# Banded attention's last output projection split by key heads around the last weighing, and the last but one unit weighed ahead of the last turns

## The chip, the cores and the metric

The kernel runs on 1 core of one Trainium2 chip. The metric is the device time of the whole program in microseconds (us). Names of engines in the profile: PE is TensorE (PEld its weight loads), DVE is VectorE, ACT is ScalarE, POOL is GpSimd, SP is SyncE, which here only issues DMAs. Each engine works off its own list of instructions, one after the other; instructions wait on semaphores for results of other engines.

## The reference

A two layer transformer on 512 tokens of width 1024, in f32. Layer 0 has differential attention, layer 1 banded attention with sinks (window 128, 16 query heads in groups of 4 on 4 key heads), and each is followed by a SwiGLU of hidden width 2816. The change lies where layer 1's attention ends and its SwiGLU begins:

```python
p = e / (jnp.sum(e, axis=-1, keepdims=True) + jnp.exp(sink - m))
o = jnp.einsum('bnhgqk,bnkhd->bnqhgd', p.astype(vw.dtype), vw)
return o.reshape(B, S, SW_HEADS * HEAD_DIM) @ w_o
...
        x = x + swiglu(rms_norm(x, ffn_norm[l]), w_gate_up[l], w_down[l])
```

## The kernel before

**Products in three passes.** Every f32 operand is split into a rounded half `hi` (an ACT cast) and the rest `lo` (a DVE subtraction), and a product is three matmuls: hi by hi, hi by lo, lo by hi (`mm3`, L295 to L298). `split_evac` (L300) does that for a PSUM result: `ph`/`pl`, `oh`/`ol`, `hTh`/`hTl` are such pairs.

**Tiling.** The 512 tokens are four tiles t = 0 to 3 of 128. Banded attention is done in 16 units; a unit is one token tile with one key head (four query heads). Units 14 and 15 belong to token tile 3, with key heads 2 and 3. A unit has five steps: `turn_q` (transpose the queries), `score` (scores, softmax; L1395), `turn_p` for two key blocks (L1432: four PE transposes of the weights `s` into a `tr` bank, then ACT's `ph` and DVE's `pl`), and `weigh` (L1445: 12 matmuls of 256 columns into the only `po` bank, six for each key block, then `oh` by ACT and `ol` by DVE). `po` has one bank, so a weighing cannot start before the `ol` of the one ahead of it has read it.

**Output projection.** `o_block` (L457) adds one token tile's share of `o @ w_o` to the residual `xs`: for each of two column halves n it runs j = 0 to 3 (three matmuls of 512 columns each) into one `acc` bank and then adds the bank to `xs` on DVE (L468). j = 0 and 1 read the `oh`/`ol` of one unit, j = 2 and 3 those of the next: in the last call (`o_sw(1, 3)`, chunk 1, token tile 3) j = 0, 1 are unit 14's and j = 2, 3 are unit 15's. Its weights are four units of two `hi`/`lo` tiles, which fill the eight buffers that the pool has (`HLB`, L44).

**The SwiGLU's start.** `ffn.norm(t)` (L520) squares `xs` on ACT with a row sum (`xn<-xs`, L526), takes the inverse root on DVE by a chain of tiny instructions (`fss`, `rsq`, `frr`) and scales into `xn` (L532). `ffn.turn(t)` (L535) transposes `xn` in two banks of four PE transposes (L314) and splits each into the token tile's columns of `hTh`/`hTl`. `ffn.start` (L594) loads gate and up weights of the first column block: four `raw` loads of 512 KB by SP into two `raw` buffers (`RAWB`, L43), each split into two `hi`/`lo` pairs (ACT L269, DVE L270), the third load waiting until the first buffer has been split. Then come the products of tokens 0 to 255 with `hTh`/`hTl` (256 columns, so token tiles 0 and 1), later those of tokens 256 to 511; `turn(2)` and `turn(3)` stand ahead of the second and the fourth group of 24 matmuls.

**Order of the work.** PE's list is in the order of the code (`manual_schedule`). The steps of units are sorted by the times in `SW_AT` (L117), and projections of finished tiles fill between them (`fill.pull`, L1510). What is left of the fill comes at `fill.drain()` (L1521), then the last projection with `ffn.turn(0)` after its second and `ffn.turn(1)` after its sixth of eight (n, j) steps, then `ffn.start`. The lists of ACT, DVE and SP are put in order by a scheduler with priorities: `high_priority(offset=HOT)` moves the norm and the additions to `xs` far forward, the splits less far.

Of the kernel before, what the change touches and what calls it, by code (L numbers as in the profile page):

```python
# [13 lines left out]
ALU = mybir.AluOpType  # L14
# [26 lines left out]
HOT = 1220  # L41
# [72 lines left out]

DA_FILL3 = 0.4757
SW_K = [11.4, 13, 18.5, 22]
SW_AT = [11.99, 12, 15.9293, 17.8936, 24.5, 15.49, 15.5, 20.5, 21.3936, 26, 19.99, 20, 25, 26, 28.8496, 24.49, 24.5, 29.5, 30.5, 33.0389, 25.6, 29.3765, 35.7519, 36, 38.8496, 28.8, 30.9738, 38.2, 40.3017, 42.0496, 32, 34.1738, 41.4, 43.5017, 45.2496, 36.9539, 39.3779, 46.3539, 48.4383, 50.2036, 45.6745, 48.0985, 55.0745, 57.0527, 58.1744, 47.0802, 52.5434, 56.4802, 57.4802, 60.3298, 50.3802, 54.7802, 59.7802, 60.7802, 63.6298, 53.6802, 58.0802, 63.0802, 64.0802, 66.9298, 57.032, 60.327, 66.3802, 67.3802, 70.2298, 60.4435, 63.7903, 69.8435, 70.8435, 72.7553, 65.4286, 69.8286, 74.8286, 75.8286, 77.7403, 67.7612, 72.1612, 77.6383, 78.1612, 80.073]  # L117
SW_R = [24.5925, 29, 34.7335, 50, 54, 60.3794]
SW_F = 57.2488
SW_BOOST = 51  # L120
# [17 lines left out]
def tile_yoco_hybrid(  # L138
# [24 lines left out]
    nc = tc.nc  # L163
    count = [0]

    def nm(s):
        count[0] += 1
        return f"{s}_{count[0]}"
# [12 lines left out]
    def acc():  # L181
        return ps.tile([P, 512], F32, name=nm("acc"), tag="acc", bufs=4)

    def att(tag="tr"):
        return ps.tile([P, 512], F32, name=nm(tag), tag=tag, bufs=3 if tag == "tr" else 1)
# [7 lines left out]
    xs = xp.tile([P, NT, D], F32, name="xs")  # L193
# [101 lines left out]
    def mm3(dst, sh, sl, mh, ml, start, stop):  # L295
        nc.tensor.matmul(dst, sh, mh, start=start, stop=False)  # L296
        nc.tensor.matmul(dst, sh, ml, start=False, stop=False)  # L297
        nc.tensor.matmul(dst, sl, mh, start=False, stop=stop)  # L298

    def split_evac(hi, lo, src):  # L300
        with tc.high_priority(offset=pri["evac"]):
            nc.scalar.copy(hi, src)
            nc.vector.tensor_tensor(lo, src, hi.bitcast(F32), op=ALU.subtract)

    def new_hT():
        hh = xp.tile([P, KT, S], F32R, name=nm("hTh"), tag="hTh", bufs=1)
        hl = xp.tile([P, KT, S], F32R, name=nm("hTl"), tag="hTl", bufs=1)
        return hh, hl

    def transpose_in(hT, src, t, h):  # L310
        pt = att()
        for j in range(4):
            k = 4 * h + j
            nc.tensor.transpose(pt[:, j * P:(j + 1) * P], src[:, k * P:(k + 1) * P], ident)  # L314
        sl = (slice(None), slice(4 * h, 4 * h + 4), slice(t * P, (t + 1) * P))
        split_evac(hT[0][sl], hT[1][sl], pt.rearrange("p (j q) -> p j q", q=P))
# [112 lines left out]
    def q_evac(ap, pt):  # L429
        q = [ap.tile([P, 256], F32R, name=nm("q"), tag=f"q{z}", bufs=QB) for z in "hl"]  # L430
        split_evac(*q, pt[:, 0:256])
        return q
# [19 lines left out]
    def o_units(w, k0):  # L452
        wv = w.rearrange("(k p) n -> p k n", p=P)
        return {(j, n): load_w([wv[:, k0 + j:k0 + j + 2, n * 512:(n + 1) * 512]], 2, 512)
                for j in (0, 2) for n in range(2)}

    def o_block(units, pieces, t, ready=None):  # L457
        while ready and not ready():
            yield None
        for n in range(2):  # L460
            pt = acc()
            for j in range(4):
                sh, sl = pieces(j, t)
                mm3(pt, sh, sl, *units[j - j % 2, n].row(j % 2), j == 0, j == 3)
                yield 0.65
            xsl = xs[:, t, n * 512:(n + 1) * 512]
            with tc.high_priority(offset=HOT):
                nc.vector.tensor_tensor(xsl, xsl, pt, op=ALU.add)  # L468


    class Flow:
# [521 lines left out]
    class Pair:  # L993
# [105 lines left out]
        def turn(self, i, h):  # L1099
            hf = i // 2  # L1100
            if (hf, h) not in self.aT:
                self.aT[hf, h] = [[self.ap.tile([P, 2, 256], F32R, name=nm("aT"), tag=f"aT{e}", bufs=4)
                                   for _ in range(1 + hf)] for e in range(2)]
            th, tl = self.aT[hf, h]
            pt = att()
            src = self.sb[i][h]
            for j in range(i + 1):
                nc.tensor.transpose(pt[:, j * P:(j + 1) * P], src[:, 0, j * P:(j + 1) * P], ident)
            for jp in range(0, i + 1, 2):
                w = min(2, i + 1 - jp)  # L1110
                sl = (slice(None), slice(0, w), slice((i % 2) * P, (i % 2) * P + P))
                split_evac(th[jp // 2][sl], tl[jp // 2][sl],
                           pt[:, jp * P:(jp + w) * P].rearrange("p (j q) -> p j q", q=P))

        def weigh(self, hf, h):
            if h == 0:
                self.po = att("po")
            po, vs = self.po, self.vs
            th, tl = self.aT[hf, h]
            nj = 2 + 2 * hf  # L1120
            for j in range(nj):
                c0 = P if j == nj - 1 else 0
                mm3(po[:, h * 256 + c0:(h + 1) * 256],
                    vs[j][0][:, h * P:(h + 1) * P], vs[j][1][:, h * P:(h + 1) * P],
                    th[j // 2][:, j % 2, c0:256], tl[j // 2][:, j % 2, c0:256], j == 0, j == nj - 1)
            if h == 1:
                self.osb = self.ap.tile([P, 512], F32, name=nm("osb"), tag="osb", bufs=1)
                with tc.high_priority(offset=pri["evac"]):
                    nc.scalar.copy(self.osb, po)
                self.osq = self.ap.tile([P, 512], F32, name=nm("osq"), tag="u", bufs=3)  # L1130
                nc.scalar.activation(self.osq, self.osb, AF.Square)
# [29 lines left out]
    with tc.tile_pool(name="da", bufs=1, reuse_waits="tile") as ap:  # L1161
# [84 lines left out]
        for p in range(4):  # L1246
# [8 lines left out]
            else:  # L1255
                fill = Fill([o_da(0, range(NT)), o_da(1, range(2), lambda: 0 in pairs[3].outs)])
                each = DA_FILL3
                ffn = Ffn(0, ap)
# [34 lines left out]
    with tc.tile_pool(name="sw", bufs=1, reuse_waits="tile") as ap:  # L1293
# [92 lines left out]
        def place(u):  # L1386
            i, kk = divmod(u - 8, 2) if u >= 8 else (u % 4, 0)
            s, kv = ("C", 2 + kk) if u >= 8 else ("AB"[u // 4], u // 4)
            return s, i, kk, kv, ((i - 1, i) if i else (0,))
# [37 lines left out]
                nc.scalar.activation(sb[:, g, 0:n], sb[:, g, 0:n], AF.Copy, scale=rs[:, g:g + 1])  # L1427
            soft[u] = sb

        pT, soft, kdone, vdone = {}, {}, set(), set()  # L1430

        def turn_p(u, b):  # L1432
            s, i, kk, kv, blocks = place(u)
            if b >= len(blocks):
                return
            pt = att()
            for g in range(4):
                col = (g % 2) * 256 + (g // 2) * P
                nc.tensor.transpose(pt[:, col:col + P], soft[u][:, g, b * P:(b + 1) * P], ident)
            ph = ap.tile([P, 512], F32R, name=nm("ph"), tag="ph", bufs=2)  # L1440
            pl = ap.tile([P, 512], F32R, name=nm("pl"), tag="pl", bufs=2)
            split_evac(ph, pl, pt)
            pT[u, b] = (ph, pl)

        def weigh(u):  # L1445
# [16 lines left out]
        def pieces_sw(ch):  # L1462
            return lambda j, t: tuple(z[:, j % 2, :] for z in o_all[2 * ch + j // 2, t])

        sw_units = {}

        def o_sw(ch, t):
            while (2 * ch + 1, t) not in o_all:
                yield None
            if ch not in sw_units:  # L1470
                sw_units[ch] = o_units(sw_w_o[0], 4 * ch)
            yield from o_block(sw_units[ch], pieces_sw(ch), t)
            if ch:
                ffn.norm(t)

        def hook(k, t):
# [22 lines left out]
        todo = [(at, t, turn_a) for t, at in enumerate(SW_K)]  # L1499
        for u in range(16):  # L1500
            for n, f in enumerate((turn_q, score, turn_p, turn_p, weigh)):
                if u >= 4 or n:
                    todo.append((SW_AT[5 * u + n], u, f) + ((n - 2,) if n in (2, 3) else ()))
        todo += [(at, *z, q_rope) for at, z in zip(SW_R, (("B", 1), ("B", 2), ("B", 3), ("C", 1), ("C", 2), ("C", 3)))]
        todo.append((SW_F, Ffn))
        fill = Fill([gemm(units_of((wqv, 256, gq), (wkv, 256, gkv)), hT, 512, 2, b_post),
                     gemm(units_of((wqv, 512, gq)), hT, 512, 2, c_post)]
                    + [o_sw(0, t) for t in range(NT)] + [o_sw(1, t) for t in range(NT - 1)])
        now = 0.0
        for at, *z in sorted(todo, key=lambda z: z[0]):  # L1510
            fill.pull(at - now)
            now = at
            if z[0] is Ffn:
                ffn = Ffn(1, ap)
# [4 lines left out]
            else:  # L1519
                z[1](z[0], *z[2:])  # L1520
        fill.drain()  # L1521
        for n, _ in enumerate(o_sw(1, 3)):
            if n == 1:
                ffn.turn(0)
            if n == 5:
                ffn.turn(1)
        ffn.start({1: lambda: ffn.turn(2), 3: lambda: ffn.turn(3)})

    with tc.tile_pool(name="ffn1", bufs=1, reuse_waits="tile") as fp:
# [37 lines left out]
```

## Time and profile before

| | |
|---|---|
| median of 3 runs | 1122.76 us (1122.44 to 1123.15) |
| the profiled execution's own time | 1122.68 us |
| its span, first to last instruction | 1120.6 us |
| what lies around the span | 2.08 us |
| mean granted TensorE clock | 0.998 |
| busy: PE, DVE, ACT | 1101.9, 1007.9, 709.4 us |

The profile shows one execution. A row of a timeline has the start in us from the span's start, the time of the instruction (of several together, with x4), the engine, the line, the operation with out<-in, and in brackets how long the engine stood idle before it and what ended that. A matmul's time overlaps the next one's: what a matmul costs on PE is the distance of the starts.

### The profile page before, as it was taken

The page shows a single profiled execution, that of the slowest core. Times are in us where ns is not written, and L with a number is a line of the kernel's source. Part 1 is how long each engine was busy: PE and PEld are TensorE (multiplying, and loading weights), DVE is VectorE, ACT ScalarE, POOL GpSimd, SP SyncE. Part 2 cuts the span into 40 slices and gives each one's busy share as a digit, 9 for nine tenths or more (in the row PEclk, how much of TensorE's full clock was granted, in tenths as well). Part 3 has the DMA queues.
Part 4 walks back from the last instruction along what each step waited for, and adds up shares of the span by engine and source line. Part 5 has one row for each costly group of instructions (what it writes and reads, how often), then busy time and mean ns, then how long its engine had stood idle before and what let it go on. Part 6 is the DMA issues. An engine that isn't in the chain of part 4 may idle for free.

```text
span 1120.6 us, 20161 instructions
## 1 busy us (share of the span) xinstructions
PE 1101.9 (98%) x7206; PEld 979.5 (87%) x7206; DVE 1007.9 (90%) x2418; ACT 709.4 (63%) x1575; POOL 54.6 (5%) x76
## 2 busy tenths in 40 slices
PE   9999999999999999999999999999999999999998
PEld 7878888778989989989998778778989999998997
DVE  5979798979999999999998787988899999899997
ACT  5565756454556675675677499697555675566574
POOL 0100000000000010010003000000010000000000
PEclk9999999999999999999999999999999999999999
DMA  6312121224453444336124311120545247246213
GB/s 199 113 57 76 39 77 48 67 69 137 151 158 100 143 87 156 114 84 199 58 48 106 112 39 57 39 76 26 198 136 168 76 104 213 79 104 178 77 30 103
DMA packets 94085, 114.90 MB, mean 103 GB/s; under 512 B 5993, under 2 KB 70914, under 8 KB 93986
## 3 DMA queue, kind: packets, MB, share of 16 engines
q1 hardware_dynamic: 87216, 100.97, 28.0%
q0 software_dynamic: 6720, 12.65, 6.3%
q8 instruction: 56, 0.92, 0.3%
q14 instruction: 43, 0.35, 0.1%
q10 hardware_dynamic: 50, 0.01, 0.0%
HBM read 99.98 MB, written 2.10 MB: 91 GB/s over the span
## 4 chain that ended last, share of the span: by engine, by line
PE 81%; DVE 12%; ACT 6%; issue 1%; POOL 0%; DVEq 0%; ACTq 0%; POOLq 0%
PE acc L725 18%; PE tr L725 12%; PE tr L813 10%; PE acc L813 8%; PE acc L296 8%; PE acc L297 7%; PE acc L298 7%; PE po L725 2%; ACT s L1420 2%; PE tr L439 2%; DVE hss L389 1%; ACT s L1427 1%; DVE lo L270 1%; DVE u L405 1%; PE po L813 1%
## 5 line engine op out<-in xcount | busy, mean ns | idle before, releaser
L589 ACT CAST hi<-r 128x512 fp32r<-128x512 f32 x160 | 98.9, 620 | 78.9 <-PE acc L725 34.2
L296 PE MATMUL acc<-hi,hTh 128*128 128x512 f32 (+1 forms) x352 | 133.1, 378 | 2.2 <-DVE vl L1029 2.2
L297 PE MATMUL acc<-lo,hTh 128*128 128x512 f32 (+1 forms) x352 | 124.4, 354 | 0.4 <-DVE lo L270 0.4
L298 PE MATMUL acc<-hi,hTl 128*128 128x512 f32 (+1 forms) x352 | 124.4, 354 | 0.0
L589 ACT CAST hi<-g 128x512 fp32r<-128x512 f32 x154 | 94.9, 618 | 40.6 <-PE acc L297 19.2
L591 DVE TENSOR_TENSOR lo<-r,hi 128x512 fp32r<-128x512 f32 x160 | 104.8, 685 | 5.8 <-ACT hi L589 5.4
L589 ACT CAST hi<-raw 128x512 fp32r<-128x512 f32 x108 | 66.9, 620 | 61.5 <-PE tr L725 19.0
L796 ACT CAST ah<-lf 128x256 fp32r<-128x256 f32 x154 | 61.2, 404 | 47.2 <-PE tr L813 14.7
L725 PE MATMUL acc<-hTh,lo 128*128 128x256 f32 x288 | 81.5, 283 | 0.0
L725 PE MATMUL acc<-hTl,hi 128*128 128x256 f32 x288 | 81.5, 283 | 0.0
L725 PE MATMUL acc<-hTh,hi 128*128 128x256 f32 x288 | 81.4, 283 | 0.0
L725 PE MATMUL acc<-tl,hi 128*128 128x256 f32 x288 | 81.1, 282 | 0.0
L725 PE MATMUL acc<-th,hi 128*128 128x256 f32 x288 | 81.1, 281 | 0.0
L725 PE MATMUL acc<-th,lo 128*128 128x256 f32 x288 | 81.0, 281 | 0.0
L296 PEld LDWEIGHTS acc<-hi,hTh 128*128 128x128 f32 x352 | 66.9, 190 | 12.9 <-issue 2.6
L269 ACT CAST hi<-raw 128x512 fp32r<-128x512 f32 x96 | 57.4, 619 | 30.8 <-PE acc L298 17.6
L591 DVE TENSOR_TENSOR lo<-g,hi 128x512 fp32r<-128x512 f32 x110 | 75.2, 684 | 1.5 <-ACT hi L589 1.4
L298 PEld LDWEIGHTS acc<-hi,hTl 128*128 128x128 f32 x352 | 66.8, 190 | 9.5
L588 POOL DMA_DIRECT2D lo<-g x44 | 38.5, 975 | 715.1 <-ACT lo L587 308.4
L297 PEld LDWEIGHTS acc<-lo,hTh 128*128 128x128 f32 x352 | 67.1, 191 | 6.7 <-DVE lo L270 0.7
L591 DVE TENSOR_TENSOR lo<-raw,hi 128x512 fp32r<-128x512 f32 x108 | 72.7, 685 | 0.0
L270 DVE TENSOR_TENSOR lo<-raw,hi 128x512 fp32r<-128x512 f32 x96 | 64.4, 684 | 6.7 <-ACT hi L269 6.3
(278 smaller groups left out, 3635.0 us busy)
## 6 DMA issues: line engine op xcount, KB each, us to landing
r<-in_w_gate_up_dram SPq DMA_DIRECT2D x80, 512.0 KB, 4.9
g<-in_w_down_dram SPq DMA_DIRECT2D x88, 256.0 KB, 5.3
lo<-g POOLq DMA_DIRECT2D x44, 256.0 KB, 3.8
raw<-in_da_w_qkv_dram SPq DMA_DIRECT2D x30, 256.0 KB, 3.1
raw<-in_da_w_qkv_dram SPq DMA_DIRECT2D x8, 512.0 KB, 4.0
raw<-in_da_w_o_dram SPq DMA_DIRECT2D x8, 512.0 KB, 3.7
raw<-in_w_gate_up_dram SPq DMA_DIRECT2D x8, 512.0 KB, 3.7
raw<-in_sw_w_o_dram SPq DMA_DIRECT2D x8, 512.0 KB, 3.7
```

Of the source, the lines that this page charges most:

```text
L269: nc.scalar.copy(hi, part)
L270: nc.vector.tensor_tensor(lo, part, hi.bitcast(F32), op=ALU.subtract)
L296: nc.tensor.matmul(dst, sh, mh, start=start, stop=False)
L297: nc.tensor.matmul(dst, sh, ml, start=False, stop=False)
L298: nc.tensor.matmul(dst, sl, mh, start=False, stop=stop)
L439: nc.tensor.matmul(banks[c][:, cols], q[a][rows], k[b][rows], start=a + b == 0, stop=a == 1)
L588: nc.gpsimd.dma_start(out=lo.bitcast(F32), in_=src, accum_op=ALU.add)
L589: nc.scalar.copy(hi, src)
L591: nc.vector.tensor_tensor(lo, src, hi.bitcast(F32), op=ALU.subtract)
L725: nc.tensor.matmul(dst, l[:, k, :], r[:, k, :], start=fresh and k == 0 and i == 0, stop=k == 3 and i == 2, skip_group_check=not fresh)
L796: nc.scalar.copy(ah, src)
L813: nc.tensor.matmul(bank, l[:, tk], r, start=fresh and i == 0 and n == 0, stop=i == len(qs) - 1 and n == 2, skip_group_check=not fresh)
```

## The change

Two things in the table and the end of the layer:

- `SW_AT`: unit 14's weighing goes from 77.7403 to 77.62, ahead of unit 15's two turns (77.6383, and 78.1612 becomes 77.64); unit 15's weighing leaves the table.
- The last projection is written as `o_block2`, which takes (n, half) pairs in the order (0,0), (1,0), (0,1), (1,1): first unit 14's half for both column halves, then unit 15's. Unit 15's weighing comes after the first pair, `norm(2)` and `turn(0)` after the second, `turn(1)` inside the fourth, one step before the end. `norm(2)` is held behind unit 15's last `ph` cast, and `norm(3)` is issued after the projection as before.

```diff
-SW_AT = [..., 65.4286, 69.8286, 74.8286, 75.8286, 77.7403, 67.7612, 72.1612, 77.6383, 78.1612, 80.073]
+SW_AT = [..., 65.4286, 69.8286, 74.8286, 75.8286, 77.62, 67.7612, 72.1612, 77.6383, 77.64, 80.073]
...
+    def o_block2(units, pieces, t, order):
+        banks = {}
+        for n, half in order:
+            if n not in banks:
+                banks[n] = acc()
+            for j in (2 * half, 2 * half + 1):
+                mm3(banks[n], *pieces(j, t), *units[2 * half, n].row(j % 2), j == 0, j == 3)
+                yield n, j
+            if half:
+                xsl = xs[:, t, n * 512:(n + 1) * 512]
+                with tc.high_priority(offset=HOT):
+                    nc.vector.tensor_tensor(xsl, xsl, banks[n], op=ALU.add)
...
-            if ch:
+            if ch and t < 2:
                 ffn.norm(t)
...
         fill.drain()
-        for n, _ in enumerate(o_sw(1, 3)):
-            if n == 1:
+        last = casts[15, 1]
+        for n, j in o_block2(sw_units[1], pieces_sw(1), 3, ((0, 0), (1, 0), (0, 1), (1, 1))):
+            if (n, j) == (0, 1):
+                weigh(15)
+            if (n, j) == (1, 1):
+                with tc.issue_after(last.ins):
+                    ffn.norm(2)
                 ffn.turn(0)
-            if n == 5:
+            if (n, j) == (1, 2):
                 ffn.turn(1)
+        ffn.norm(3)
         ffn.start({1: lambda: ffn.turn(2), 3: lambda: ffn.turn(3)})
```

On PE, `turn(1)`'s eight transposes come three matmuls of 512 columns ahead of the SwiGLU's first matmul, where six stood between them; the SwiGLU's first matmul reads `hTh`, its second `hTl`, both in the columns of token tiles 0 and 1.

What stands on DVE and ACT then, at the place where the projection ends. In all rows a number behind a name is a buffer's; `raw_10038` is the fourth and last weight load of the SwiGLU's start, `fss_9989` belongs to `norm(3)`.

On DVE, the rows up to `turn(1)`'s two `hTl` and beyond, before: the weight rests `lo` of the second load, `turn(1)`'s `hTl` (from the banks `tr_9968` and `tr_9975`), the last addition to `xs`, the third load, and then the norm of token tile 3.

```order
L270 TENSOR_TENSOR lo_10021<-raw_10018,hi_10020 128x512
L270 TENSOR_TENSOR lo_10025<-raw_10018,hi_10024 128x512
L303 TENSOR_TENSOR hTl_9616<-tr_9968,hTh_9615 128x4x128
L303 TENSOR_TENSOR hTl_9616<-tr_9975,hTh_9615 128x4x128
L468 TENSOR_TENSOR xs<-xs,acc_9961 128x512
L270 TENSOR_TENSOR lo_10031<-raw_10028,hi_10030 128x512
L270 TENSOR_TENSOR lo_10035<-raw_10028,hi_10034 128x512
L527 TENSOR_SCALAR fss_9989<-fss_9989 128x1
```

And DVE in the changed kernel, from the additions to `xs` to `turn(1)`'s two `hTl` (from `tr_9971` and `tr_9978`):

```order
L483 TENSOR_TENSOR xs<-xs,acc_9897 128x512
L483 TENSOR_TENSOR xs<-xs,acc_9921 128x512
L270 TENSOR_TENSOR lo_10031<-raw_10028,hi_10030 128x512
L270 TENSOR_TENSOR lo_10035<-raw_10028,hi_10034 128x512
L270 TENSOR_TENSOR lo_10041<-raw_10038,hi_10040 128x512
L542 TENSOR_SCALAR fss_9989<-fss_9989 128x1
L270 TENSOR_TENSOR lo_10045<-raw_10038,hi_10044 128x512
L241 TENSOR_SCALAR rsq_h_9996<-fss_9989 128x1
L242 TENSOR_SCALAR rsq_t_9995<-fss_9989 128x1
L303 TENSOR_TENSOR hTl_9616<-tr_9971,hTh_9615 128x4x128
L243 TENSOR_SCALAR rsq_s_9994<-rsq_t_9995 128x1
L303 TENSOR_TENSOR hTl_9616<-tr_9978,hTh_9615 128x4x128
```

`turn(1)`'s `hTl` has moved behind the last addition to `xs`, behind the rests of the third and fourth weight load, and behind the first rows of token tile 3's norm.

On ACT, the same stretch before: `turn(0)`'s second `hTh`, the second load's casts, `turn(1)`'s `hTh`, the third load, token tile 3's square, the fourth load.

```order
L302 CAST hTh_9615<-tr_9947 128x4x128
L269 CAST hi_10020<-raw_10018 128x512
L269 CAST hi_10024<-raw_10018 128x512
L302 CAST hTh_9615<-tr_9968 128x4x128
L302 CAST hTh_9615<-tr_9975 128x4x128
L269 CAST hi_10030<-raw_10028 128x512
L269 CAST hi_10034<-raw_10028 128x512
L526 ACTIVATE xn_9990,fss_9989<-xs 128x1024
L269 CAST hi_10040<-raw_10038 128x512
```

And ACT in the changed kernel, from token tile 2's square on:

```order
L541 ACTIVATE xn_9929,fss_9928<-xs 128x1024
L269 CAST hi_10010<-raw_10008 128x512
L269 CAST hi_10014<-raw_10008 128x512
L302 CAST oh_9917<-po_9904 128x256
...
L269 CAST hi_10030<-raw_10028 128x512
L269 CAST hi_10034<-raw_10028 128x512
L302 CAST hTh_9615<-tr_9971 128x4x128
L302 CAST hTh_9615<-tr_9978 128x4x128
L269 CAST hi_10040<-raw_10038 128x512
L269 CAST hi_10044<-raw_10038 128x512
L541 ACTIVATE xn_9990,fss_9989<-xs 128x1024
```

The third load's casts now stand ahead of `turn(1)`'s `hTh`, and the fourth load's ahead of token tile 3's square.

More of the change, by code (lines that the diff above doesn't have):

```diff
@@ L116 @@
 SW_K = [11.4, 13, 18.5, 22]
-SW_AT = [11.99, 12, 15.9293, 17.8936, 24.5, 15.49, 15.5, 20.5, 21.3936, 26, 19.99, 20, 25, 26, 28.8496, 24.49, 24.5, 29.5, 30.5, 33.0389, 25.6, 29.3765, 35.7519, 36, 38.8496, 28.8, 30.9738, 38.2, 40.3017, 42.0496, 32, 34.1738, 41.4, 43.5017, 45.2496, 36.9539, 39.3779, 46.3539, 48.4383, 50.2036, 45.6745, 48.0985, 55.0745, 57.0527, 58.1744, 47.0802, 52.5434, 56.4802, 57.4802, 60.3298, 50.3802, 54.7802, 59.7802, 60.7802, 63.6298, 53.6802, 58.0802, 63.0802, 64.0802, 66.9298, 57.032, 60.327, 66.3802, 67.3802, 70.2298, 60.4435, 63.7903, 69.8435, 70.8435, 72.7553, 65.4286, 69.8286, 74.8286, 75.8286, 77.7403, 67.7612, 72.1612, 77.6383, 78.1612, 80.073]
+SW_AT = [11.99, 12, 15.9293, 17.8936, 24.5, 15.49, 15.5, 20.5, 21.3936, 26, 19.99, 20, 25, 26, 28.8496, 24.49, 24.5, 29.5, 30.5, 33.0389, 25.6, 29.3765, 35.7519, 36, 38.8496, 28.8, 30.9738, 38.2, 40.3017, 42.0496, 32, 34.1738, 41.4, 43.5017, 45.2496, 36.9539, 39.3779, 46.3539, 48.4383, 50.2036, 45.6745, 48.0985, 55.0745, 57.0527, 58.1744, 47.0802, 52.5434, 56.4802, 57.4802, 60.3298, 50.3802, 54.7802, 59.7802, 60.7802, 63.6298, 53.6802, 58.0802, 63.0802, 64.0802, 66.9298, 57.032, 60.327, 66.3802, 67.3802, 70.2298, 60.4435, 63.7903, 69.8435, 70.8435, 72.7553, 65.4286, 69.8286, 74.8286, 75.8286, 77.62, 67.7612, 72.1612, 77.6383, 77.64, 80.073]
 SW_R = [24.5925, 29, 34.7335, 50, 54, 60.3794]
@@ L301, in split_evac @@
         with tc.high_priority(offset=pri["evac"]):
-            nc.scalar.copy(hi, src)
+            cast = nc.scalar.copy(hi, src)
             nc.vector.tensor_tensor(lo, src, hi.bitcast(F32), op=ALU.subtract)
+        return cast
     def new_hT():
@@ L1428, in score @@
             soft[u] = sb
-        pT, soft, kdone, vdone = {}, {}, set(), set()
+        pT, soft, casts, kdone, vdone = {}, {}, {}, set(), set()
         def turn_p(u, b):
@@ L1441, in turn_p @@
             pl = ap.tile([P, 512], F32R, name=nm("pl"), tag="pl", bufs=2)
-            split_evac(ph, pl, pt)
+            casts[u, b] = split_evac(ph, pl, pt)
             pT[u, b] = (ph, pl)
@@ L1501, in tile_yoco_hybrid @@
             for n, f in enumerate((turn_q, score, turn_p, turn_p, weigh)):
-                if u >= 4 or n:
+                if (u >= 4 or n) and (u, n) != (15, 4):
                     todo.append((SW_AT[5 * u + n], u, f) + ((n - 2,) if n in (2, 3) else ()))
```

## Prediction

> **What bounds the kernel now.** I read the page first, then PE's waits, then the timelines of PE, ACT, DVE and SP from 770 to 790 us, where the change lies, and last the granted clock around the longest wait.
>
> ```profile
> span 1120.6 us, 20161 instructions
> PE 1101.9 (98%) x7206; PEld 979.5 (87%) x7206; DVE 1007.9 (90%) x2418; ACT 709.4 (63%) x1575; POOL 54.6 (5%) x76
> ```
>
> PE is busy all the time, so the time is PE's work plus its stalls. PE's waits over the span: the longest, another long one, the only one behind 783 us, and the one in this stretch:
>
> ```profile
> PE acc L296 <- DVE vl L1029: 2.2, 1, 2.2
> ...
> PE tr L1439 <- DVE mx L1409: 1.4, 1, 1.4
> ...
> PE tr L813 <- ACT hi L589: 0.8, 1, 0.8
> PE po L296 <- DVE ol L303: 0.8, 1, 0.8
> ```
>
> So whatever PE loses or gains before 783 us goes into the end one to one: there is one wait left to swallow it, local to the SwiGLU's own steps. The stretch on PE:
>
> ```profile
> 770.37 1.52 PE L1439 MATMUL tr<-ident,s 128*128 128x128 f32 x4
> 771.65 0.36 PE L296 MATMUL po<-ph,vpad 128*128 128x256 f32 x1
> ...
> 772.76 0.39 PE L297 MATMUL po<-pl,vpad 128*128 128x256 f32 x1
> ...
> 773.46 0.60 PE L1439 MATMUL tr<-ident,s 128*128 128x128 f32 x4
> 774.82 0.39 PE L296 MATMUL po<-ph,vpad 128*128 128x256 f32 x1 [0.76 <-DVE ol L303]
> 775.04 0.28 PE L297 MATMUL po<-pl,vpad 128*128 128x256 f32 x1
> ...
> 776.36 0.40 PE L296 MATMUL acc<-hi,oh 128*128 128x512 f32 x1
> 776.59 0.40 PE L297 MATMUL acc<-lo,oh 128*128 128x512 f32 x1
> ...
> 781.37 1.03 PE L314 MATMUL tr<-ident,xn 128*128 128x128 f32 x8
> 782.16 0.48 PE L296 MATMUL acc<-hi,oh 128*128 128x512 f32 x1
> ...
> 783.61 0.28 PE L296 MATMUL acc<-hTh,hi 128*128 128x256 f32 x1
> 783.73 0.28 PE L297 MATMUL acc<-hTl,hi 128*128 128x256 f32 x1
> ```
>
> By distance of starts a 512-column matmul costs 0.23 us, one of 256 columns 0.12, eight transposes 0.79, so four 0.4 with what the next instruction loses behind them. Four transposes at 770.37 took 1.28 (they wait for unit 15's softmax), and weighing 15 stood 0.76 for `po`. From 783.73 PE never waits for `turn(1)`'s `hTl`. The other engines there:
>
> ```profile
> 774.10 0.59 ACT L302 CAST ph<-tr 128x512 fp32r<-128x512 f32 x1
> ...
> 782.00 1.07 ACT L302 CAST hTh<-tr 128x512 fp32r<-128x512 f32 x2 [1.18 <-PE tr L314]
> ...
> 784.54 1.06 ACT L526 ACTIVATE xn<-xs 128x1024 f32<-128x1024 f32 x1 [0.26 <-DVE xs L468]
> 785.50 0.18 ACT L526 ACTIVATION_READ_ACCUMULATOR xn<-xs 128x1 f32 x1
> 785.96 1.14 ACT L269 CAST hi<-raw 128x512 fp32r<-128x512 f32 x2 [0.27 <-DMA raw<-in_w_gate_up_dram]
> ```
>
> ```profile
> 772.01 0.69 DVE L303 TENSOR_TENSOR pl<-tr,ph 128x512 fp32r<-128x512 f32 x1 [0.78 <-ACT ph L302]
> ...
> 782.62 1.29 DVE L303 TENSOR_TENSOR hTl<-tr,hTh 128x512 fp32r<-128x512 f32 x2 [0.33 <-ACT hTh L302]
> 783.83 0.68 DVE L468 TENSOR_TENSOR xs<-xs,acc 128x512 f32<-128x512 f32 x1
> 784.42 1.29 DVE L270 TENSOR_TENSOR lo<-raw,hi 128x512 fp32r<-128x512 f32 x2
> 785.72 0.15 DVE L527 TENSOR_SCALAR fss<-fss 128x1 f32<-128x1 f32 x1
> ```
>
> The first `hTl` ran from 782.62 to about 783.30, 0.43 us before PE's matmul on it at 783.73. Token tile 3's norm (`fss`, 785.72) came 3.1 us after that `hTl` had begun. In the changed DVE list it comes before it; that is the point on which this forecast rests.
>
> **The change part by part.** PE's order is the same up to 770.37, so I count on from there.
>
> *The weighings and the split projection.* Weighing 14 now starts at 770.37, but its eighth matmul needs the second `pl`, which DVE makes from 772.01 to 772.70 as before; it ran at 772.76 and does so again, so the weighing ends at 773.46 as before. Then come both turns of unit 15, 2 x 0.4, to 774.2, six projection matmuls for unit 14 (6 x 0.23) to 775.6, and weighing 15. `po` is free by then: `oh` and `ol` of unit 14 follow 773.46 at once, to about 774.5. Its last `ph` and `pl` (ACT from 774.1 two casts of 0.5, DVE 0.6 behind) are there by 776.0, needed at 776.4. So the 0.76 wait is gone: weighing 15 ends at 775.6 + 12 x 0.12 = 777.1. What is left on PE is 18 projection matmuls (4.2, and 0.15 behind transposes) and sixteen transposes (1.6): 783.0 instead of 783.61. This part gains 0.6 to 0.7 us.
>
> *`turn(1)`'s way to the SwiGLU.* The changed lists put a chain between the projection and PE's second SwiGLU matmul. I follow it from ACT. Token tile 2's square (1.14 with its read) follows unit 15's last cast: 775.1 to 776.1 at the next instruction. Two casts of the first load at 0.52 each (half of such a pair) end at 777.2; DVE's two rests follow to about 778.1. That frees the first `raw` buffer, and SP can issue the third load. In the profile of before SP issued the third and the fourth load at
>
> ```profile
> 779.32 0.37 SPq L287 DMA_DIRECT2D raw<-in_w_gate_up_dram  x1
> ...
> 782.32 0.37 SPq L287 DMA_DIRECT2D raw<-in_w_gate_up_dram  x1
> ```
>
> and ACT, waiting for the fourth, got it at 785.96: 3.64 us. So the third load lands at about 778.1 + 3.65 = 781.8. ACT's list holds behind that wait two casts, `turn(1)`'s two `hTh`, and the fourth load's two casts: 6 x 0.52 = 3.1 to 784.9 (the fourth load, out when DVE has the second buffer's rests, by 779.8, is there at 783.5 and holds nothing). Then token tile 3's square with its read, 1.14 to 786.1; its `xs` was complete at about 783.8. DVE's list has `fss`, a rest (0.6), two tiny ones (0.2 at most) and the first `hTl` (0.68): 786.1 + 0.1 + 0.6 + 0.2 + 0.7 = 787.7. PE's second SwiGLU matmul starts at about 787.75 instead of 783.73, 4.0 us later with the gain counted in. Nothing hides it: PE's list has only SwiGLU matmuls behind it. Bounds: if no load held anything, the chain would still run from PE's last projection matmul (begun at 782.8, its result 0.4 later) over the addition (0.7), the square (1.1) and DVE's rows (1.6) to 786.6, a delay of 2.9, or 2.6 with the shortest of each. If ACT, DVE and the load are each a few tenths slower, 788.6, a delay of 4.9. I take the count, 4.0.
>
> *The restart.* Behind a wait the second matmul followed after 0.22 instead of 0.12 (774.82 to 775.04): 0.1 us.
>
> *The clock.* PE stands from 783.0 to 787.75, but for one matmul on `hTh`: 4.7 us. What a long stand does shows at the longest wait, of 2.2 us. Granted clock in the column behind PE's busy time, then matmuls before and behind it:
>
> ```profile
> 44.50:46.70 2.20, 0.04 (x2) 0.96 0.62 196
> 46.70:48.00 1.30, 1.30 (x3) 0.50 0.01 3
> ...
> 49.40:51.00 1.60, 1.60 (x9) 0.84 0.38 92
> ```
>
> ```profile
> 46.70 0.79 PE L296 MATMUL acc<-hi,hTh 128*128 128x512 f32 x1 [2.16 <-DVE vl L1029]
> ...
> 47.71 0.63 PE L298 MATMUL acc<-hi,hTl 128*128 128x512 f32 x1
> 48.14 0.63 PE L296 MATMUL acc<-hi,hTh 128*128 128x512 f32 x1
> ```
>
> The clock fell to half shortly before 46.7 (0.96 as a mean of 2.2 us is 0.18 us at half) and came back at about 49.9 (0.84 of 1.6 us is 0.5 us at half): 3.4 us. Matmuls cost 0.43 instead of 0.23 in it. If half of the clock falls on 1.4 to 3.4 us behind the restart, as the drop comes early or late in the stand, that loses 0.6 to 1.6 us; I take 1.2, near the row, where the restart came just behind the drop. [...]
>
> *Sum.* 4.0 + 0.1 + 1.2 = 5.3 us, against the profiled execution's 1122.68 (1120.6 and 2.08 around it; the median of the runs is 1122.76): **1128.0 us**.
>
> **Rivals.**
>
> *The clock stays up* (0.15): a stand drops it only in some positions, or the lone matmul on `hTh` in its first us keeps it up. Then 4.1 us: 1126.8. For it speaks the mean clock:
>
> ```profile
> core 0: 1120.6 us, clock 0.998
> ```
>
> 0.2% of 1120.6 is 2.2 us of lost clock, and the one drop seen costs 1.7 of them, so the wait of 1.4 us dropped nothing. Against it: 2.2 us were enough once. [...]
>
> *The loads are not in the way* (0.09): the third lands early, and only the projection's end binds. A delay of 2.6 to 3.1, and a clock loss of 0 to 1.2: 1125.4 to 1127.0. For it: nothing but my count puts the third load at 781.8.
>
> *The loads are slower than before* (0.08): third and fourth now go out 1.7 us apart, with SP's next loads close behind, instead of 3.0, so the fourth may land late. Each us beyond 783.9 is one more: 1129.5 to 1131.
>
> *Nothing waits for the norm* (0.05), the one on the other side: if DVE reaches `turn(1)`'s first `hTl` before about 782.9, PE's second SwiGLU matmul goes at 783.1 and only the weighing's gain is left: 1122.0, or level when the shorter way from `turn(1)` (three matmuls, 0.77 us, against 1.9 for bank, cast and rest) costs 0.3. That would need the norm's square to be done before the projection it reads; so it can only come by lists other than those shown. Against it too: DVE in the profile of before went exactly in its list's order, `hTl`, `xs`, `lo`, `lo`, `fss`.
>
> **How the numbers follow.** The forecast itself has 0.63: 1126.9 (early drop, short chain) to 1129.3 (4.9 + 0.1 + 1.6). The range for 8 in 10 takes in the rival without the clock and part of that without loads: 1126.0 to 1129.4. What a measurement can tell from no change is 0.2%, 2.25 us: slower is above 1125.0, faster below 1120.5. Slower holds all cases but the last and the lowest edge of the second: 0.92; within 0.07; faster 0.01.
>
> **What would show it.** Right: PE's waits list one of about 4 us, on the matmul `acc<-hTl,hi`, ended by DVE `hTl`; the wait on `po` for `ol` is gone; the timeline of DVE has `fss` of token tile 3 before `turn(1)`'s `hTl`; the granted clock is 0.5 for some us behind the wait. Wrong: PE's matmuls on `hTl` begin before 784 us, or the wait lies elsewhere; a PE wait behind 800 us that was not there before would mean that the delay is partly hidden, or adds to another.

## The result and the profile after

| | before | after |
|---|---|---|
| median | 1123.15 us (7 runs, 1122.29 to 1127.8) | 1130.59 us (7 runs, 1127.4 to 1131.29) |
| the profiled execution's own time, span | 1122.68, 1120.6 | 1131.07, 1129.1 |
| of the span: up to the last projection matmul of token tile 2 | 770.12 | 772.02 |
| from there to `turn(3)`'s transposes ("the stretch" below) | 22.99 | 29.87 |
| from there to the end | 327.49 | 327.21 |

The ratio is 1.0055, with a 95% interval of 1.0038 to 1.0072: on 1122.76 us that is 6.2 us slower (4.3 to 8.1), 1128.9 us. The forecast was 1128.0 (1126.0 to 1129.4). The median of the seven runs of the change, 1130.59, lies 1.2 us above that range, and the profiled execution's own time, 1131.07, lies 1.7 above it.

The stretch begins where both kernels have still done the same on PE and ends behind the last place where the change is felt. The 1.90 us that the profiled execution loses ahead of it lie in instructions that the change doesn't touch (PE's order is the same up to there). So I compare stretches, and of the whole program only ratios.

Of the profile after, first the core's span and clock, then PE's waits from 765 us to the end:

```profile
core 0: 1129.1 us, clock 0.995
```

```profile
PE acc L297 <- DVE rsq_s L243: 4.3, 1, 4.3
PE po L296 <- ACT ph L302: 0.6, 1, 0.6
PE po L297 <- DVE pl L303: 0.3, 1, 0.3
PE acc L296 <- ACT hTh L302: 0.3, 1, 0.3
```

One wait of 4.3 us has come, on the SwiGLU's second matmul (below, PE "stands" means that it waits idle). The wait on `po` for `ol` is gone; the two `po` waits listed now are weighing 14's, for its second `ph` and `pl`; that time was spent before inside the four transposes that took 1.28 us. The 0.8 us wait behind 800 us that the profile of before had is not listed here, yet the rest of the span is only 0.28 us shorter.

PE around the wait:

```profile
784.72 0.40 PE L298 MATMUL acc<-hi,ol 128*128 128x512 f32 x1
785.45 0.39 PE L296 MATMUL acc<-hTh,hi 128*128 128x256 f32 x1 [0.33 <-ACT hTh L302]
790.13 0.58 PE L297 MATMUL acc<-hTl,hi 128*128 128x256 f32 x1 [4.29 <-DVE rsq_s L243]
790.51 0.41 PE L298 MATMUL acc<-hTh,lo 128*128 128x256 f32 x1
...
794.99 0.41 PE L298 MATMUL acc<-hTh,lo 128*128 128x256 f32 x1
795.20 1.10 PE L315 MATMUL tr<-ident,xn 128*128 128x128 f32 x8
...
796.49 0.28 PE L296 MATMUL acc<-hTh,hi 128*128 128x256 f32 x1
796.61 0.28 PE L297 MATMUL acc<-hTl,hi 128*128 128x256 f32 x1
```

The projection's last matmul starts 12.70 us into the stretch (before: 783.39 - 770.12 = 13.27), the first on `hTl` at 18.11 (before 13.61). Behind it the starts are 0.21 us apart up to 795.20, and 0.12 later. ACT in that time:

```profile
783.77 1.14 ACT L269 CAST hi<-raw 128x512 fp32r<-128x512 f32 x2 [1.53 <-DMA raw<-in_w_gate_up_dram]
784.82 1.06 ACT L302 CAST hTh<-tr 128x512 fp32r<-128x512 f32 x2
786.38 1.14 ACT L269 CAST hi<-raw 128x512 fp32r<-128x512 f32 x2 [0.49 <-DMA raw<-in_w_gate_up_dram]
787.42 1.05 ACT L541 ACTIVATE xn<-xs 128x1024 f32<-128x1024 f32 x1
788.38 0.19 ACT L541 ACTIVATION_READ_ACCUMULATOR xn<-xs 128x1 f32 x1
```

And DVE:

```profile
785.89 1.89 DVE L270 TENSOR_TENSOR lo<-raw,hi 128x512 fp32r<-128x512 f32 x3
788.60 0.15 DVE L542 TENSOR_SCALAR fss<-fss 128x1 f32<-128x1 f32 x1 [0.82 <-ACT xn L541]
788.67 0.68 DVE L270 TENSOR_TENSOR lo<-raw,hi 128x512 fp32r<-128x512 f32 x1
...
789.39 0.68 DVE L303 TENSOR_TENSOR hTl<-tr,hTh 128x512 fp32r<-128x512 f32 x1
789.99 0.14 DVE L243 TENSOR_SCALAR rsq_s<-rsq_t 128x1 int32<-128x1 int32 x1
```

The chain is the one in the lists: third load, `hTh`, fourth load, token tile 3's square, `fss`, a rest, `hTl`, and only then PE. The profile names `rsq_s` as PE's releaser because that tiny row begins just where `hTl` ends (789.99 and 789.39 + 0.6); the matmul reads `hTl`. `turn(1)`'s `hTh` was there by 785.9, so the stand belongs to `hTl` alone.

The granted clock (the column behind PE's busy time, then DMA share and GB/s):

```profile
787.00:788.00 1.00, 0.00 (x0) 1.00 1.08 385
788.00:790.00 2.00, 0.00 (x0) 0.62 1.09 386
790.00:795.00 5.00, 4.87 (x23) 0.50 1.08 390
795.00:796.00 1.00, 1.00 (x9) 0.84 1.05 406
```

It fell to half at about 788.5 (0.62 as a mean of 2 us is 1.52 us at half) and came back at about 795.3: 6.8 us, twice the 3.4 us seen before.

### The profile page after: what moved, and what is told of

It reads as the page before. It is cut to its first block, busy times and chain, and to the rows that moved or that the text cites. A ratio compares the mean times of both kernels' runs of the same rounds, so it can differ in the third digit from the quotient of the medians.

```text
span 1129.1 us, 20162 instructions
## 1 busy us (share of the span) xinstructions
PE 1105.5 (98%) x7206; PEld 982.5 (87%) x7206; DVE 1008.4 (89%) x2418; ACT 709.7 (63%) x1575; POOL 54.6 (5%) x76
## 4 chain that ended last, share of the span: by engine, by line
PE 78%; DVE 13%; ACT 6%; issue 1%; DMA 1%; POOL 0%; DVEq 0%; ACTq 0%; POOLq 0%
PE acc L740 18%; PE tr L740 11%; PE tr L828 9%; PE acc L828 8%; PE acc L296 7%; PE acc L297 7%; PE acc L298 7%; PE po L740 2%; ACT s L1435 2%; PE tr L440 2%; DVE lo L270 2%; DVE hss L390 1%; ACT s L1442 1%; DVE u L406 1%; PE po L828 1%
```

## The experiments

Theory: DVE's and ACT's lists hold `turn(1)`'s `hTl` behind the loads' halves and token tile 3's norm, PE stands for it, and the stand halves the clock. Rivals: the norm alone binds, the loads alone bind, the distance of three matmuls between `turn(1)` and the SwiGLU is too short, or PE is slow behind the wait because weight loads stream at the same time (DMA share 1.08), not because it stood. Each table row gives the starts, in us into the stretch, of the last projection matmul and of the first SwiGLU matmul on `hTl`, then the length of the stretch, all three from the one profiled execution, and last the ratio of the runs (4 to 12 of each kernel) to runs of before taken beside them.

| kernel | last proj. | `hTl` | stretch | ratio (95%) |
|---|---|---|---|---|
| before | 13.27 | 13.61 | 22.99 | |
| the change | 12.70 | 18.11 | 29.87 | 1.0055 (1.0038 to 1.0072) |
| norm behind `turn(1)` | 12.70 | 18.16 | 29.02 | 1.0063 (1.0048 to 1.0078) |
| `turn(1)` first | 12.70 | 14.28 | 23.76 | 1.0010 (1.0001 to 1.0019) |
| loads 3, 4 behind `turn(1)` | 12.68 | 14.59 | 24.05 | 1.0017 (1.0008 to 1.0027) |
| 42 transposes, lists moved | 12.67 | 17.62 | 27.00 | 1.0026 (1.0016 to 1.0035) |
| 44 transposes, same lists | 12.70 | 18.70 | 28.17 | 1.0030 (1.0020 to 1.0040) |
| `turn(1)` a step earlier | 12.71 | 18.88 | 30.59 | 1.0048 (1.0030 to 1.0066) |
| casts and rests first | 12.70 | 13.04 | 22.42 | 0.9991 (0.9981 to 1.0001) |
| and the old table | 12.56 | 12.90 | 22.28 | 0.9987 (0.9979 to 0.9996) |

### Only the norm out of the way

`norm(3)` is held behind `turn(1)`'s last `hTl` (`rest` collects the DVE rests of `split_evac`).

```diff
-        ffn.norm(3)
+        with tc.issue_after(rest[-1].ins):
+            ffn.norm(3)
```

> The changed kernel, with norm(3) put behind turn(1)'s last hTl on DVE; the rests of the third and fourth weight load still stand ahead of that hTl. Measured from the last projection matmul of token tile 2 to turn(3)'s transposes, before takes 22.99 us and the change 29.87. Theory of the lists (everything ahead of hTl on DVE counts, the loads as well as the norm): the wait for hTl shrinks from 4.3 us by 1 to 1.5 only, since the fourth load still lands where it did, PE still stands over 3 us, the clock still drops: 27.5 to 29 us, and 1127 to 1129 us in all. Rival, the norm alone holds hTl: the wait is gone or under 0.5 us, 22.4 to 23.5, and about 1122.5 in all.

The time is that of the change, 1.0063, and the stretch of 29.02 lies just above the 27.5 to 29 expected: the wait did not shrink, but it did not vanish either, as the rival would have it. PE's two waits, and then the loads: ACT's row and the time from issue to landing.

```profile
PE acc L297 <- DVE hTl L303: 2.5, 1, 2.5
PE acc L296 <- ACT hTh L302: 2.1, 1, 2.1
```

```profile
784.48 1.14 ACT L269 CAST hi<-raw 128x512 fp32r<-128x512 f32 x2 [3.32 <-DMA raw<-in_w_gate_up_dram]
```

```profile
DMA to landing us min/median/max: 4.6/5.0/5.3
```

`hTl` now comes ahead of `fss`, and still PE stands 4.7 us: here the loads' casts and rests alone make the chain that long. The third load took 5.3 us against the 3.5 of the change, so ACT stood 3.32 us for it and passed the wait on to `hTh`. So the norm is not what binds alone. What it adds in the change can be estimated from the part of the chain behind the third load: from the start of ACT's casts of the fourth load to PE's matmul on `hTl` it takes 2.61 us here (786.48 to 789.09) and 3.75 us in the change (786.38 to 790.13), so the norm adds about 1.1 us there. That is an estimate, for the loads landed differently in the two profiled executions. The lost time behind the restart is 29.02 - 18.16 = 10.86 against 9.38 before (22.99 - 13.61): 1.48 us, with the clock down for 3.4 us (0.71 as the mean of 788 to 790, 0.50 up to 792, 0.94 up to 794: from 788.84 to 792.24) instead of 6.8.

### `turn(1)` ahead on DVE

```diff
-                ffn.turn(1)
+                with tc.high_priority(offset=HOT):
+                    ffn.turn(1)
```

> The changed kernel, with turn(1) in the high priority of the additions: on DVE its two hTl now stand between the two additions to xs, ahead of all rests of the third and fourth load and of norm(3); on ACT its hTh stays behind the third load's casts. Theory of the lists: PE's wait for hTl falls from 4.3 us to 0.5 to 1, the clock does not drop, the stretch that is 22.99 us before and 29.87 in the change is 23.2 to 24; in all 0 to +1 us against before. Rival, that the split projection itself costs (the way from turn(1) to the SwiGLU is now only three matmuls): a wait of 2 us or more stays, over 25 us.

Of the 6.88 us, 6.11 are gone. DVE and PE of this kernel:

```profile
783.92 1.29 DVE L303 TENSOR_TENSOR hTl<-tr,hTh 128x512 fp32r<-128x512 f32 x2 [0.19 <-ACT hTh L302]
785.12 0.68 DVE L483 TENSOR_TENSOR xs<-xs,acc 128x512 f32<-128x512 f32 x1
```

```profile
783.93 0.39 PE L296 MATMUL acc<-hTh,hi 128*128 128x256 f32 x1 [0.46 <-ACT hTh L302]
784.66 0.39 PE L297 MATMUL acc<-hTl,hi 128*128 128x256 f32 x1 [0.34 <-DVE hTl L303]
```

With `hTl` ahead of the rests and of the last addition, the stand shrinks to 0.46 and 0.34, and the clock stays at 1.00. What is left is `turn(1)`'s cast on ACT, which still stands behind the third load's casts.

### The last two loads' halves behind `turn(1)`

The rests (and so what follows from them) of loads 3 and 4 are held behind `turn(1)`'s last `hTl`.

```diff
+                if b and held:
+                    behind.append(held)
...
-        ffn.start({1: lambda: ffn.turn(2), 3: lambda: ffn.turn(3)})
+        held = rest[-1].ins
+        ffn.start({1: lambda: ffn.turn(2), 3: lambda: ffn.turn(3)}, held)
```

> The changed kernel, with the third and fourth load's rests held behind turn(1)'s last hTl on DVE; norm(3) falls behind it with them, both additions to xs stay ahead of it. ACT's list is as in the change, so turn(1)'s hTh still waits behind the casts of the third load. Theory of the lists: hTl comes right behind the second addition to xs, PE's wait is 1 to 1.5 us, the clock stays up, the stretch (22.99 before, 29.87 changed) is 23.8 to 24.5; in all +0.8 to +1.5 us against before. Rival, the transfer of the loads is what is late, not the list: the wait stays over 3 us.

24.05, with waits of 0.5 (`hTh`) and 0.6 us (`hTl`) and a clock of 1.00. DVE then:

```profile
785.05 1.28 DVE L303 TENSOR_TENSOR hTl<-tr,hTh 128x512 fp32r<-128x512 f32 x2
786.25 0.68 DVE L270 TENSOR_TENSOR lo<-raw,hi 128x512 fp32r<-128x512 f32 x1
788.56 0.15 DVE L542 TENSOR_SCALAR fss<-fss 128x1 f32<-128x1 f32 x1 [1.62 <-ACT xn L541]
```

The norm's `fss` is behind `hTl` here too, by itself. In the first experiment it was behind as well, with the loads ahead: `hTl`'s matmul comes at 18.16 there and at 14.59 here, so 3.6 us of its delay are the loads. Not all of this is their place in the list: ACT got the third load 13.55 us into the stretch there and 11.90 here, so 1.65 of the 3.6 are that load's later landing, and about 1.9 are the rests ahead of `hTl`. What the norm alone would cost, ahead of `hTl` with the loads behind it, was not tried.

### PE kept busy, first try

42 transposes whose result nothing reads stand between `norm(3)` and the SwiGLU.

```diff
         ffn.norm(3)
+        busy(42)
```

> The changed kernel with 42 transposes of the identity into the po bank between the projection and the SwiGLU, whose result nobody reads, so that PE works through most of its wait for hTl. The wait's cause is untouched. Theory (of the 6.9 us lost in the stretch, 4.5 are the wait and 2.4 the clock that drops because PE stands): hTl comes at the same time, 18.1 us into the stretch, the clock stays at 1.00 behind it, the stretch is 27.4 to 27.8 instead of 29.87, and the whole 2 to 2.5 us shorter than the change. Rival, matmuls behind the wait are slow because of the loads that stream in then: 29.5 or more, and still 0.21 us per 256-column matmul.

This did something else than meant. The added instructions moved the priorities of all that follows, and DVE's list with them:

```profile
784.27 1.27 DVE L483 TENSOR_TENSOR xs<-xs,acc 128x512 f32<-128x512 f32 x2
785.46 1.28 DVE L303 TENSOR_TENSOR hTl<-tr,hTh 128x512 fp32r<-128x512 f32 x2
786.66 0.68 DVE L270 TENSOR_TENSOR lo<-raw,hi 128x512 fp32r<-128x512 f32 x1
```

`hTl` went ahead of the rests, so PE was held by the 42 transposes alone and not by `hTl`. The run says nothing on the length of the wait. It does say that loads streaming beside PE at this rate don't slow it here: the rows below have DMA share and clock of this kernel behind the restart, where the stretch's end comes 27.00 - 17.62 = 9.38 us behind the matmul on `hTl`, as before (busy time of PE, PEld, DVE, ACT and POOL, then clock, DMA share and GB/s):

```profile
788.00:794.00 6.00, 6.00 (x54) 6.00 (x53) 4.63 (x15) 2.20 (x5) 0.00 (x0) 1.00 1.09 390
```

### PE kept busy, with the lists of the change

44 transposes, and the splits' priorities moved by as much, so that the lists of the other engines are those of the change.

```diff
         ffn.norm(3)
+        busy(44)
+        pri['boost'] += 44
         ffn.start({1: lambda: ffn.turn(2), 3: lambda: ffn.turn(3)})
+        pri['boost'] -= 44
```

> The changed kernel with 44 transposes of the identity into the po bank behind the projection, as in the run with 42 of them, but with the loads' priority raised by as much, so that ACT's and DVE's lists are those of the changed kernel row for row and hTl comes as late as there. Theory (4.5 us of the wait, 2.4 of the clock): PE's first matmul on hTl stays at about 18.1 us into the stretch, within 0.5 for the loads, the clock stays at 1.00, matmuls of 256 columns cost 0.12 us, the stretch is 27.3 to 28 (before 22.99, changed 29.87). Rival, the slow matmuls come from something else than PE's standing: the clock is 0.5 again and the stretch 29.5 or more.

PE and the clock:

```profile
787.13 0.36 PE L296 MATMUL acc<-hTh,hi 128*128 128x256 f32 x1
788.17 0.39 PE L297 MATMUL acc<-hTl,hi 128*128 128x256 f32 x1 [0.68 <-DVE rsq_s L243]
788.39 0.28 PE L298 MATMUL acc<-hTh,lo 128*128 128x256 f32 x1
788.51 0.27 PE L296 MATMUL acc<-hTh,hi 128*128 128x256 f32 x1
```

```profile
786.00:788.00 2.00, 1.49 (x14) 1.00 1.09 386
788.00:790.00 2.00, 1.83 (x15) 1.00 1.09 379
```

The wait for `hTl` still ends late, 18.70 us into the stretch (0.6 later than in the change and just over the 0.5 allowed for the loads, as the third load reached ACT 0.6 later), but PE had work nearly up to it: the clock stays at 1.00 and the matmuls are 0.12 us apart. From there to the stretch's end it is 28.17 - 18.70 = 9.47 us, against 11.76 in the change and 9.38 before. So the clock costs the change 2.3 us, and only because PE stood. The stretch, 28.17, is longer than the 27.3 to 28 expected by about as much as `hTl` came later.

### `turn(1)` one step earlier on PE

Six matmuls of 512 columns between `turn(1)` and the SwiGLU, as before; the other engines' lists stay as in the change.

```diff
-            if (n, j) == (1, 2):
+            if (n, j) == (0, 3):
```

> The changed kernel with turn(1)'s transposes one projection step earlier on PE, so that six matmuls stand between them and the SwiGLU, as before the change. ACT's and DVE's lists keep the order of the changed kernel. Theory of the lists: nothing is gained, the wait for hTl is 4 us or more, the stretch 29 to 30.5. Rival, the shorter way on PE (three matmuls instead of six) is what makes hTl late: the wait goes to 0 to 0.3 us, the stretch to 22.3 to 23.

```profile
PE acc L297 <- DVE rsq_s L243: 5.0, 1, 5.0
```

30.59, just above the 29 to 30.5 expected: the distance on PE does nothing as long as DVE's list is what it is. The `hTl` rows start where the list lets them, and the fourth load was later still (ACT stood 1.64 us for the third and 1.16 us for the fourth).

### `turn(1)` first on ACT and DVE

This is "casts and rests first" in the table: `turn(1)` a step earlier and at a higher priority, and the casts of loads 3 and 4 held behind its last cast on ACT, so that neither list has a load ahead of it (`cast_of` collects the casts of `split_evac`).

```diff
-            if (n, j) == (1, 2):
-                ffn.turn(1)
+            if (n, j) == (0, 3):
+                with tc.high_priority(offset=2 * HOT):
+                    ffn.turn(1)
+                held = cast_of[-1].ins
...
-        ffn.start({1: lambda: ffn.turn(2), 3: lambda: ffn.turn(3)})
+        ffn.start({1: lambda: ffn.turn(2), 3: lambda: ffn.turn(3)}, held)
```

> The changed kernel with turn(1) one projection step earlier, in twice the additions' priority, and the third and fourth load's casts held behind its last hTh: ACT has hTh ahead of the loads, DVE has hTl ahead of the additions to xs, of the loads' rests and of norm(3). Theory: no wait for hTl, the 0.55 to 0.65 us that the split projection takes off PE are left, first matmul on hTl at 12.9 to 13.2 us instead of 13.61, the stretch 22.2 to 22.6; in all 0.4 to 0.7 us under before, which the times may not tell from no change. Rival, the split costs elsewhere: 23 or more.

```profile
782.95 0.39 PE L298 MATMUL acc<-hi,ol 128*128 128x512 f32 x1
783.18 0.28 PE L296 MATMUL acc<-hTh,hi 128*128 128x256 f32 x1
783.29 0.28 PE L297 MATMUL acc<-hTl,hi 128*128 128x256 f32 x1
```

No wait is left at the SwiGLU, and the split projection keeps what it gains: the stretch is 22.42, 0.57 us under before, which is just the 13.27 - 12.70 of the last projection matmul. The ratio, 0.9991, has 1 in its interval (up to 1.0001).

### And the old table

The same with the three numbers of `SW_AT` as before, so that unit 14's weighing comes behind unit 15's turns again.

> As the run with casts and rests first, but with unit 14's weighing back between unit 15's two turns (the three numbers of the table as before the change). PE then has transposes to do while weighing 14 waits for its second ph and pl. Theory: the end of weighing 14 is set by that pl either way, so one group of four transposes (0.36 us) comes off PE's path: the stretch 21.8 to 22.3. Rival, the change of the table is worth its place (weighing 14 early frees po for weighing 15): 22.4 or more.

From 765 to 815 us PE has no listed wait at all, and the last projection matmul comes at 12.56. So the table's share is a loss of 0.14 us, not the 0.36 of a group of transposes that was expected, and less than the 0.63 + 0.34 of weighing 14's waits, for most of that time was spent in slow transposes before. The stretch is 22.28, 0.71 under before; the ratio is 0.9987 (0.9979 to 0.9996), 0.4 to 2.4 us on 1122.76. This is the version whose interval lies clear of both kernels, if by little. The runs don't tell it from the kernel before it (medians of 1122.64 and 1122.68): that the old table is the better one rests on the stretch of one execution each.

## Why the prediction was right, and where its sizes were off

- **Direction and mechanism: right.** The wait of about 4 us on `acc<-hTl,hi`, `fss` ahead of `hTl` on DVE, the `po` wait for `ol` gone, the clock at 0.50 behind the wait: all in the profile. The two list experiments that move `hTl` ahead take 6.11 and 5.82 of the 6.88 us away, and the one that puts `hTh` and `hTl` ahead takes away all of it. One sign was named too narrowly: the releaser in the list is `rsq_s`, the row that begins as `hTl` ends.
- **The split projection: right, and a little smaller.** 0.57 us against "0.6 to 0.7"; weighing 14 waits openly, and it ends as late as before.
- **The wait: 4.50 us instead of 4.0.** The count held up to the third load, which landed as counted: 783.77 less the 1.90 us of drift is 781.87, against 781.8. The step that failed is "the fourth load [...] is there at 783.5 and holds nothing": on the same scale ACT got it at 784.48, after standing 0.49 us, and the square, `fss` and `hTl` followed that much later. It went out 0.3 us later than the 779.8 counted (782.03 less 1.90), and took 0.7 us longer to land. The loads' landing times were 3.6 to 3.8 us before, with issues 3.0 us apart, and 3.5 and 4.3 with the two 1.9 us apart:

```profile
DMA to landing us min/median/max: 3.5/3.9/4.3
```

  The rival "the loads are slower than before" named such a late fourth load, and its number fits: 784.48 is 0.58 behind its 783.9, and ACT stood 0.49. It had a chance of 0.08 and was priced at 1129.5 or more; a part of it belonged into the sum.
- **Restart and clock: 2.38 us instead of 0.1 + 1.2.** This is the term that was mis-sized most, and it lies outside its bound of 1.6. That half of the clock lasts 3.4 us was read from one case in which PE worked through nearly all of these 3.4 us (3.22 of them). Here the clock fell at 788.5 while PE still stood until 790.13, so PE was busy for only half of the first 3.4 us (1.78 us); the clock stayed at half for twice as long, 6.8 us, and 5.1 us of work ran at half of the clock. The experiment that keeps PE busy puts the price at 2.3 us. The slow stretch was 3.4 us where PE restarted 0.2 to 0.3 us behind the drop (46.51 to 46.70 in before, 788.84 to 789.09 with the norm behind `turn(1)`) and 6.8 where it restarted 1.6 to 1.7 behind it (788.50 to 790.13 here, 788.64 to 790.38 with `turn(1)` a step earlier). The count had only the first case to go by. "The clock stays up" was the rival, and it fell.
- **Sum.** 4.50 + 2.38 = 6.88 in the stretch, against 5.3. The ratio's 6.2 us (4.3 to 8.1) holds both. Two terms were too small, both in the same direction: 6.88 on the 1122.68 of the profiled execution would be 1129.6, just above the range. That the ratio's 1128.9 lies inside is in part luck.
- **What stays open.** Why the third load took over 5 us in two kernels (norm behind `turn(1)`; casts and rests first) and 3.5 to 4.1 in the others; and what one of the change's seven runs, at 1127.4 us with a mean clock of 0.998, did not lose: 3.4 us at half make 0.998 in before, 3.4 and 6.8 make 0.995 in the change, but this run's stretch was not seen.

## What to carry to other kernels

Moving a step on the bound engine also moves where its helpers stand in the lists of the other engines; read these lists in the changed kernel from the moved step to its first reader, and look for a DMA, or an instruction that depends on the result still being computed, ahead of it. A gain of half a us on PE was worth nothing while `hTl` stood behind two loads, and was all there when the reader's inputs were put first. A stand of 2.2 us or more on PE should be priced with the clock behind it: here one of 2.2 us brought 3.4 us at half of the clock (before) or none (44 transposes), and those of 4.3 and 5.0 us brought 6.8. The stands of 0.3 to 0.7 us at the SwiGLU's start (`turn(1)` first, loads behind `turn(1)`, 44 transposes) brought none, the clock there stayed at 1.00 (the next section has more numbers).

## What was not expected of the hardware

**The same wait halves the clock in one execution and not in another.** The wait for `vl` early in the program took 2.16 us in before, 2.21 in the change and 2.20 in the kernel with 44 transposes. In before, and with 44 transposes, from 40 to 52 us:

```profile
40.00:52.00 12.00, 9.84 (x57) 0.86 0.43 132
```

```profile
40.00:52.00 12.00, 9.80 (x63) 1.00 0.41 129
```

With 0.86 as the mean of 12 us, the first lost 1.7 us; the second lost none, with the same wait of 2.2 us. Nor does the clock fall at the same point of the wait. Before, and then the change:

```profile
46.00:47.00 1.00, 0.30 (x1) 0.75 0.22 77
47.00:50.00 3.00, 3.00 (x10) 0.51 0.00 0
```

```profile
46.00:47.00 1.00, 0.16 (x1) 1.00 0.17 60
47.00:50.00 3.00, 3.00 (x11) 0.63 0.00 0
```

In before the clock fell at 46.51, 1.97 us behind the start of the wait and 0.19 us ahead of PE's restart at 46.70. In the change it fell at 47.81, 3.17 us behind the start of the wait and 0.97 us behind the restart at 46.84, with PE at work. Both times it stayed at half for 3.41 us. The late drops came 2.66 us behind the start of the wait for `hTl` in the change (785.84 to 788.50), 2.3 with the norm behind `turn(1)` (786.54 to 788.84) and 3.2 with `turn(1)` a step earlier (785.43 to 788.64). The 1.8 us wait at the program's start (before and the change, clock 1.00 from 0 to 44 us) and the 1.4 us wait on `mx` (clock 1.00 from 52 to 780 us) brought no drop. So waits of up to 1.8 us brought no drop here, those of 2.5 (right behind one of 2.1), 4.3 and 5.0 us did, and one of 2.2 us went either way; what decides that, and when the clock falls, these runs do not show.

The spread between runs goes with the mean clock: of the 27 runs of before beside the last four experiments, the eight with a mean clock of 1.000 have a median span of 1120.25 us, the eighteen with 0.998 one of 1121.8. The 1.55 us between them are near the 1.7 of the one drop in the profile of before; whether the eighteen had that drop was not seen.

**Loads issued closer together took longer.** The same 512 KB load took 3.5 to 5.4 us from issue to landing. Where the third and fourth were issued 3.0 us apart (before) the slower took 3.8 us; in the eight kernels with 1.8 to 1.9 us between them the slower took 4.3 to 5.4, and in the one with 2.2 us (the old table) 4.1. That the spacing is the cause is not shown, for no run changed it alone. The longer landing hurt only where something stood behind the loads in a list: in the kernel with casts and rests first the slower took 5.4 us and PE waited for no load.
